# DeltaNet decays from shared operands: the sums of g, and the causal mask added in PSUM

## The chip, the cores and the metric

The kernel runs on one core of one Trainium2 chip. The metric is the device time of one execution in microseconds; the time of a kernel is the median of its runs.

## The reference

Two layers over 512 positions of width 1024, all in float32. Layer 0 mixes tokens with gated DeltaNet, layer 1 with a convolution module; each layer then attends to a memory of 256 positions and applies an MLP of width 4096. Only the gates and decays of the DeltaNet layer are changed:

```python
proj = h @ w_in                                   # q, k, v, z and 2 x 8 columns b_raw, a_raw
beta = jax.nn.sigmoid(b_raw)
g = -jnp.exp(a_log) * jax.nn.softplus(a_raw + dt_bias)     # log-decay, one per position and head
g_cum = jnp.cumsum(g, axis=-1)                    # within a chunk
diff = g_cum[..., :, None] - g_cum[..., None, :]
decay = jnp.exp(jnp.where(causal, diff, -jnp.inf))
lower = jnp.where(strict, einsum(k_beta, k) * decay, 0.0)   # I + lower is then solved
attn_intra = einsum(q, k) * decay
```

There are eight heads of width 128. The kernel works with chunks of 128 positions, four for each head.

## The kernel before, in words

Activations lie transposed: 128 channels on the partitions, 512 positions along the free axis. A large product in near-float32 precision is three matmuls of type float32r: each operand is split into a high and a low part (`h`, `l`), and `mm3` (lines 218 to 222) adds high x high, high x low and low x high in PSUM. Weights arrive by DMA as `raw` tiles of 128x1024; `wsplit` casts the high part `wh` on ScalarE (ACT) and subtracts the low part `wl` on VectorE (DVE).

The DeltaNet layer is written as a list `mains` of matmul pieces, most of 12 matmuls (half of one 128-column block of the projection), in the order `DN_ORDER`: k, q, z, v of heads 0 to 3, then of heads 4 to 7. `S.at(i, rank, f)` hangs side work on a piece `i`, and `run` emits it after that piece. The numbers at the end of the file (`T_STAT`, `T_DEC`, `K2`, `Q2`, `FS`, `DEC1`) say at which piece. The framework then orders each engine's instructions anew from this program, so an edit can move neighbours that it does not name. Each engine takes its own queue strictly in order.

The steps around the change:

- `mm_ab` (line 1112) interleaves the projection of the first k head with the 16 columns of alpha and beta: for each of 8 input tiles three matmuls of 512 columns for the head and three with 16 weight columns (`abh`, `abl`).
- `Norm.square`, `stat`, `spread`: the sum of squares over the channels (`sq` on DVE, `ssq` on TensorE), its root on ACT, and its spread `rb` over all partitions. All evictions of the projections multiply by `rb`.
- `gates` (line 338): `ab` times `rb`, four transposes to positions on the partitions, then some twenty small steps on DVE and three exponentials on ACT that give `g` and `beta`, 128x32 (8 heads x 4 chunks).
- `decay_in` (line 386): for each head GpSimd (POOL) forms `gi` = the triangle times `g`, 128x512; ACT and DVE split it into `gih` and `gil`.
- `decay` (line 393): for each head two matmuls of the other triangle with `gih` and `gil` give the sums of g between two positions; ACT takes the exponential, POOL sets the part above the diagonal to zero with a second product with the triangle. The result is `DtM[h]`, tile `dt`.
- `conv_head` (line 410): each head of q, k and v is multiplied by `rb` (`cv`, DVE), convolved over four positions (`cva`, by ACT, DVE, and with `cvq` also POOL), and goes through a silu on ACT (line 426).
- `k2` (line 434): transposes and the Gram matrix G of a k head; `bt` = G times the decay (DVE), scaled by `s_all` on POOL. `fs_in` gathers the diagonal blocks of `bt` into `DB` (ACT).
- `q2`, `q3`: the product of k and q times the decay (in place in `dt`), and the squares `sqq` of q for its norm.
- `fs_begin`, `fs_steps`, `fs_end`: for a group of four heads a transpose `FT` of `DB`, 31 dependent steps of forward substitution on DVE, and two transposes `TB`, `UB`.
- `mg_pre` to `mg_end`: the blocks are merged to full inverses (`mg`), with copies by ACT (`x0`) and POOL (`u0`).
- `rec`, `o_gate`, `o_norm`: the recurrence over the four chunks.

All PSUM tiles share eight banks, all 128x512 working tiles share `NSLOT` = 66 buffers. Small tiles come from the pool `sp`.

Of the kernel before, what the change touches and what calls it, by code (L numbers as in the profile page):

```python
# [8 lines left out]
F32 = mybir.dt.float32  # L9
# [5 lines left out]
P = 128  # L15
# [25 lines left out]
def tile_trunk(ctx, tc, xT, memT, prm_d, adt_d, bdw_d, fin_d, w_ab, w_kq, w_v, w_z, w_dno, w_pw1, w_pw2,  # L41
# [7 lines left out]
    up = ctx.enter_context(tc.tile_pool(name="up", bufs=NSLOT))  # L49
    sp = ctx.enter_context(tc.tile_pool(name="sp", bufs=16))  # L50
    psp = ctx.enter_context(tc.tile_pool(name="psp", bufs=8, space=bass.MemoryType.PSUM))
# [16 lines left out]
    def const(shape, s, dt=F32):  # L68
        return cp.tile(list(shape), dt, tag=s, name=s)

    def tt(e, o, a, b, op):
        e.tensor_tensor(out=o, in0=a, in1=b, op=op)  # L72
# [46 lines left out]
    for i in range(WARM):  # L119
# [6 lines left out]
                       base=0, channel_multiplier=1)  # L126
    tri_gt_r = const([P, P], "tri_gt_r", F32R)
    act.copy(tri_gt_r, tri_gt)
    ident4 = const([P, 32], "ident4")
# [197 lines left out]
    class DeltaNet:  # L327
        def __init__(self, norm):
            self.n, self.xs = norm, norm.xs
            for n, s in ((64, "abt"), (32, "beta"), (32, "g"), (96, "egd"), (32, "sek"), (32, "nk"),  # L330
                         (32, "s_all"), (32, "sdec"), (32, "s_neg"), (32, "sdec_neg"), (32, "ssq"), (4, "tok")):
                setattr(self, s, keepc(n, s))
            for s in ("GI", "DtM", "KT", "Kt", "Ai", "QT", "BT", "U", "VT", "VB", "Z", "OG", "ps", "M"):
                setattr(self, s, {})
# [50 lines left out]

        def decay_in(self, hs):
            for h in hs:
                gi = slot(s="gi")
                tt(pool, c4(gi), over_c(tri_le), over_i(self.g[:, h * 4:h * 4 + 4]), ALU.mult)
                self.GI[h] = split(gi, "gi")  # L390

        def decay(self, hs):
# [6 lines left out]
            for h in hs:  # L399
                gh, gl = self.GI.pop(h)  # L400
                ps = psum("dt")
                pe.matmul(ps, tri_gt_r, gh, start=True, stop=False)
                pe.matmul(ps, tri_gt_r, gl, start=False, stop=True)
                dt = slot(s="dt")
                act.activation(dt, ps, AF.Exp)
                tt(pool, c4(dt), c4(dt), over_c(tri_le), ALU.mult)
                self.DtM[h] = dt
# [687 lines left out]
    for b in range(4):  # L1095
        bs = slice(32 * b, 32 * b + 32)
        pool.tensor_copy(ident4[bs, :], ident[bs, bs])
    abh, abl = const([P, P], "abh", F32R), const([P, P], "abl", F32R)
    act.copy(abh, wab)
    tt(dve, abl, wab, abh.bitcast(F32), ALU.subtract)  # L1100
    n0 = Norm("dn_norm", eng=dve)
# [10 lines left out]
    def mm_ab():  # L1112
        w = wnext(("k", 0), 0)
        D.ps["ab"], D.ps["k", 0] = psum("ab"), psum("h")
        for k in range(KT):
            mm3(D.ps["k", 0], wk(w, k), n0.xs[k], k == 0, k == KT - 1)
            c = slice(16 * k, 16 * k + 16)
            mm3(D.ps["ab"][0:16, :], (abh[:, c], abl[:, c]), n0.xs[k], k == 0, k == KT - 1)

# [170 lines left out]
T_STAT = 2  # L1290
T_DEC = 10
NW = 3
# [110 lines left out]
```

## Time and profile before

| | us |
|---|---|
| median of 3 runs | 1588.56 (1587.7 to 1592.16) |
| profiled execution, its own time | 1589.25 |
| its span | 1587.5 |
| TensorE busy in the span | 1541.6 |
| DVE, ACT, POOL busy | 907.0, 656.9, 263.5 |

A line of a timeline has the start and length in us, the engine, the line of the kernel, the operation, the tile written and the tiles read, their shapes, how many such instructions are merged, and in brackets the time for which the engine was idle just before, with the instruction that ended that wait. A line of a group has the count, the busy time and the mean length in ns of one. Buffer numbers are left out of tile names. A row of stretches has the length, then for each engine its busy time and the number of its instructions, then the clock that TensorE was granted as a share of full speed, the busy share of the DMA engines and the GB/s that they moved.

### The profile page before, as it was taken

Reading aid. Unit: us, or ns where it says so; the run is one execution under the profiler, and the core shown is the slowest. Engines: PE = TensorE matmul, PEld = TensorE weight load, DVE = VectorE, ACT = ScalarE, POOL = GpSimd, SP = SyncE. Lnnn points to the kernel's source line nnn. Section 1 sums busy time; section 2 is a strip of 40 time slices with the busy share of each in tenths; the row PEclk is TensorE's granted clock in tenths of the full one; section 3 lists DMA queues with packets and bytes.
Section 4 is the critical chain, followed back from the end, with each engine's and each line's share of the span. In section 5 each row is a group of like instructions: output and inputs, shape, how many; then the busy total and the mean of one; then the engine's idle time right before and its main releaser. Section 6 shows DMA issues by size and latency. Waiting matters only on the chain.

```text
span 1587.5 us, 19586 instructions
## 1 busy us (share of the span) xinstructions
PE 1541.6 (97%) x7696; PEld 1298.6 (82%) x7696; DVE 907.0 (57%) x1288; ACT 656.9 (41%) x1004; POOL 263.5 (17%) x298
## 2 busy tenths in 40 slices
PE   9998997899999999999999999999999999999998
PEld 6777876798888888888888889888888888888886
DVE  6886878566455444343445599984545443443441
ACT  6656573745344443241324321173444432322332
POOL 1526333502111100000021316202012000000000
PEclk9999999899999999999999999999999999999999
DMA  5221113153222222322232422243212222223231
GB/s 180 67 73 60 54 42 105 52 175 107 93 66 67 87 100 93 104 96 93 96 104 93 137 88 91 73 164 101 85 41 93 93 98 101 94 93 105 95 106 53
DMA packets 46699, 147.57 MB, mean 93 GB/s; under 512 B 6288, under 2 KB 8976, under 8 KB 46608
## 3 DMA queue, kind: packets, MB, share of 16 engines
q1 hardware_dynamic: 46608, 146.33, 27.4%
q8 instruction: 60, 0.98, 0.2%
q14 instruction: 31, 0.25, 0.1%
HBM read 142.90 MB, written 2.10 MB: 91 GB/s over the span
## 4 chain that ended last, share of the span: by engine, by line
PE 85%; DVE 7%; ACT 3%; POOL 2%; issue 2%; DMA 0%; SPq 0%; DVEq 0%; POOLq 0%; ACTq 0%
PE up L220 7%; PE up L222 7%; PE up L221 7%; PE dn L220 6%; PE dn L222 6%; PE dn L221 6%; DVE ca L75 3%; PE q L220 2%; PE xo L221 2%; PE q L222 2%; PE q L221 2%; PE xo L222 2%; PE xo L220 2%; PE h L221 2%; PE pw L220 2%; PE pw L221 2%
## 5 line engine op out<-in xcount | busy, mean ns | idle before, releaser
L204 ACT CAST wh<-raw 128x1024 fp32r<-128x1024 f32 x248 | 260.5, 1052 | 705.8 <-PE dn L221 190.4
L72 DVE TENSOR_TENSOR wl<-raw,wh 128x1024 fp32r<-128x1024 f32 x248 | 312.1, 1260 | 129.7 <-ACT wh L204 123.9
L220 PE MATMUL up<-xh,wh 128*128 128x512 f32 x512 | 200.2, 391 | 0.0
L222 PE MATMUL up<-xh,wl 128*128 128x512 f32 x512 | 199.2, 389 | 0.0
L221 PE MATMUL up<-xl,wh 128*128 128x512 f32 x512 | 199.2, 389 | 0.0
L222 PE MATMUL dn<-uh,wl 128*128 128x512 f32 x448 | 174.3, 389 | 0.0
L220 PE MATMUL dn<-uh,wh 128*128 128x512 f32 x448 | 174.3, 389 | 0.0
L221 PE MATMUL dn<-ul,wh 128*128 128x512 f32 x448 | 174.3, 389 | 0.0
L72 DVE TENSOR_TENSOR h<-dn,h 128x512 f32<-128x512 f32 x56 | 41.8, 747 | 165.2 <-PE dn L222 165.2
L75 DVE SCALAR_TENSOR_TENSOR rl<-up,rb 128x512 f32<-128x512 f32 x64 | 44.2, 691 | 156.9 <-PE up L222 156.9
L72 POOL TENSOR_TENSOR tap<-ident,prm 128x512 f32<-128x512 f32 x45 | 61.9, 1406 | 329.6 <-PE up L222 263.8
L221 PEld LDWEIGHTS up<-xl,wh 128*128 128x128 f32 x512 | 96.1, 188 | 20.3 <-issue 0.5
L220 PEld LDWEIGHTS up<-xh,wh 128*128 128x128 f32 x512 | 96.1, 188 | 20.3 <-issue 0.5
L222 PEld LDWEIGHTS up<-xh,wl 128*128 128x128 f32 x512 | 96.1, 188 | 20.1
L222 PEld LDWEIGHTS dn<-uh,wl 128*128 128x128 f32 x448 | 84.1, 188 | 17.5
L220 PEld LDWEIGHTS dn<-uh,wh 128*128 128x128 f32 x448 | 84.1, 188 | 17.4
L221 PEld LDWEIGHTS dn<-ul,wh 128*128 128x128 f32 x448 | 84.1, 188 | 17.4
L72 POOL TENSOR_TENSOR sq<-sq,sq 128x512 f32<-128x512 f32 x30 | 49.9, 1664 | 252.7 <-ACT sq L295 167.8
L75 DVE SCALAR_TENSOR_TENSOR ca<-x,prm,ca 128x512 f32<-128x512 f32 x90 | 81.8, 910 | 2.1
L220 PE MATMUL h<-xh,wh 128*128 128x512 f32 x192 | 77.4, 403 | 2.1 <-ACT xh L288 2.1
L221 PE MATMUL h<-xl,wh 128*128 128x512 f32 x192 | 75.8, 395 | 0.6 <-DVE xl L75 0.6
L222 PE MATMUL h<-xh,wl 128*128 128x512 f32 x192 | 75.3, 392 | 0.0
(321 smaller groups left out, 3109.4 us busy)
## 6 DMA issues: line engine op xcount, KB each, us to landing
raw<-w_up SPq DMA_DIRECT2D x64, 512.0 KB, 3.4
raw<-w_dn SPq DMA_DIRECT2D x64, 512.0 KB, 3.5
raw<-w_pw SPq DMA_DIRECT2D x24, 512.0 KB, 3.5
raw<-w_kq SPq DMA_DIRECT2D x16, 512.0 KB, 3.6
raw<-w_k SPq DMA_DIRECT2D x16, 512.0 KB, 3.5
raw<-w_vv SPq DMA_DIRECT2D x16, 512.0 KB, 3.6
raw<-w_q SPq DMA_DIRECT2D x16, 512.0 KB, 3.4
raw<-w_o SPq DMA_DIRECT2D x16, 512.0 KB, 3.5
```

The source lines that it names most:

```text
L72: e.tensor_tensor(out=o, in0=a, in1=b, op=op)
L75: dve.scalar_tensor_tensor(out=o, in0=a, scalar=s, in1=b, op0=op0, op1=op1)
L204: act.copy(h, raw)
L220: pe.matmul(ps, wh, xh, start=first, stop=False)
L221: pe.matmul(ps, wh, xl, start=False, stop=False)
L222: pe.matmul(ps, wl, xh, start=False, stop=last)
```

## The change

*Decays.* The triangle product for each head goes, and with it `gi`, `gih`, `gil` and the mask product. One product of all heads' g with a triangle whose columns are taken relative to column 63 (`tri_mid`) gives the sums of g, head and chunk on the partitions, four copies one below the other; they are split into a float32r part and a rest (`V`). From `V` come one operand `R` for all heads (each chunk's sums, beside a pattern of ones) and one operand `L` for each group of four heads (a pattern that selects the head, beside the negative sums). The constant parts of `R` and `L` are copied on POOL (`decay_const`), the others written by DVE. For each head TensorE first writes -1e30 above the diagonal into PSUM (the identity times `later`, repeated for four chunks), then adds the product of the head's 128 columns of `L` with `R`; the exponential follows as before and gives zero above the diagonal. The first decays are emitted one piece later (`T_DEC` 11 instead of 10).

*Alpha and beta.* High and low weights stand side by side in one operand of 32 columns (`abp`): two matmuls for each input tile instead of three. The two halves of the result are added after the transposes.

The pool of small tiles has 13 buffers instead of 16.

```diff
-    sp = ctx.enter_context(tc.tile_pool(name="sp", bufs=16))
+    sp = ctx.enter_context(tc.tile_pool(name="sp", bufs=13))
...
-    tri_gt_r = const([P, P], "tri_gt_r", F32R)
-    act.copy(tri_gt_r, tri_gt)
+    ident_r = const([P, P], "ident_r", F32R)
+    act.copy(ident_r, ident)
+    later = const([P, P], "later", F32R)
+    ts(pool, later, tri_le, 1.0, ALU.subtract, 1e30, ALU.mult)
+    tri_mid = const([P, P], "tri_mid")
+    ts(pool, tri_mid, tri_le, tri_le[:, 63:64], ALU.subtract)
+    ind = const([P, 4], "ind")
+    dve.tensor_reduce(out=ind, in_=ident.rearrange("p (x c) -> p c x", c=4), op=ALU.add, axis=AX.X)
+    headm = const([P, 8], "headm")
+    headx = const([P, 32], "headx")
+    dve.tensor_reduce(out=headx, in_=ident.rearrange("p (x c) -> p x c", c=4), op=ALU.add, axis=AX.X)
+    dve.tensor_reduce(out=headm, in_=headx.rearrange("p (a h) -> p h a", h=8), op=ALU.add, axis=AX.X)
...
-            tt(dve, ab[0:16, :], self.ps.pop("ab")[0:16, :], rb[0:16, :], ALU.mult)
+            tt(dve, ab[0:32, :], self.ps.pop("ab")[0:32, :], rb[0:32, :], ALU.mult)
...
-                pe.transpose(ps_t[:, c * 16:(c + 1) * 16], ab[0:16, c * P:(c + 1) * P], ident[0:16, 0:16])
+                pe.transpose(ps_t[:, c * 32:(c + 1) * 32], ab[0:32, c * P:(c + 1) * P], ident[0:32, 0:32])
...
-            dve.tensor_copy(abt.rearrange("p (x c) -> p x c", c=4),
-                            ps_t[:, 0:64].rearrange("p (c x) -> p x c", c=4))
+            abp = ps_t[:, 0:128].rearrange("p (c x) -> p x c", c=4)
+            a3 = abt.rearrange("p (x c) -> p x c", c=4)
+            dve.tensor_copy(a3, abp[:, 16:32])
+            tt(dve, a3, abp[:, 0:16], a3, ALU.add)
...
-        def decay_in(self, hs):
-            for h in hs:
-                gi = slot(s="gi")
-                tt(pool, c4(gi), over_c(tri_le), over_i(self.g[:, h * 4:h * 4 + 4]), ALU.mult)
-                self.GI[h] = split(gi, "gi")
+        def decay_const(self, gq):
+            if gq == 0:
+                self.R = slot(F32R, "R")
+                pool.tensor_copy(c4(self.R)[64:128], over_i(ind)[64:128])
+            self.L[gq] = slot(F32R, "L")
+            pool.tensor_copy(c4(self.L[gq])[0:64], over_i(headm[:, 4 * gq:4 * gq + 4])[0:64])
+
+        def decay_sums(self):
+            grep = slot(s="grep")[:, 0:P]
+            dve.tensor_copy(grep.rearrange("p (a x) -> p a x", a=4), over_c(self.g))
+            ps = psum("ct")
+            pe.matmul(ps[:, 0:P], grep, tri_mid, start=True, stop=True)
+            v = self.V
+            act.copy(v, ps[:, 0:P])
+            for a in (1, 3):
+                rs = slice(32 * a, 32 * a + 32)
+                tt(dve, v[rs], ps[rs, 0:P], v[rs].bitcast(F32), ALU.subtract)
+            tt(dve, c4(self.R)[0:64], over_c(v.bitcast(F32))[0:64], over_i(ind)[0:64], ALU.mult)
+
+        def decay_in(self, gq):
+            stt(c4(self.L[gq])[64:128], over_c(self.V.bitcast(F32))[64:128], -1.0,
+                over_i(headm[:, 4 * gq:4 * gq + 4])[64:128], ALU.mult, ALU.mult)
...
-                gh, gl = self.GI.pop(h)
                 ps = psum("dt")
-                pe.matmul(ps, tri_gt_r, gh, start=True, stop=False)
-                pe.matmul(ps, tri_gt_r, gl, start=False, stop=True)
+                pe.matmul(c4(ps), ident_r, over_c(later), start=True, stop=False)
+                pe.matmul(ps, self.L[h // 4][:, h % 4 * P:h % 4 * P + P], self.R, start=False, stop=True)
                 dt = slot(s="dt")
                 act.activation(dt, ps, AF.Exp)
-                tt(pool, c4(dt), c4(dt), over_c(tri_le), ALU.mult)
                 self.DtM[h] = dt
...
-            mm3(D.ps["ab"][0:16, :], (abh[:, c], abl[:, c]), n0.xs[k], k == 0, k == KT - 1)
+            xh, xl = n0.xs[k]
+            pe.matmul(D.ps["ab"][0:32, :], abp[:, 32 * k:32 * k + 32], xh, start=k == 0, stop=False)
+            pe.matmul(D.ps["ab"][0:16, :], abp[:, 32 * k:32 * k + 16], xl, start=False, stop=k == KT - 1)
...
-    S.at(T_STAT + 5, 5, D.decay_in, [0, 1, 2, 3])
+    S.at(0, 4, D.decay_const, 0)
+    S.at(T_DEC - 1, 2, D.decay_sums)
+    S.at(T_DEC - 1, 3, D.decay_in, 0)
     S.at(T_DEC, 2, D.decay, [0, 1])
     S.at(T_DEC + 1, 2, D.decay, [2, 3])
+    S.at(DEC1[0] - 2, 5, D.decay_const, 1)
+    S.at(DEC1[0], 5, D.decay_in, 1)
     for i, hh in enumerate(([4, 5], [6, 7])):
-        S.at(DEC1[i], 5, D.decay_in, hh)
         S.at(DEC1[i] + 2, 2, D.decay, hh)
...
-T_DEC = 10
+T_DEC = 11
```

More of the change, by code (lines that the diff above doesn't have):

```diff
@@ L332, in __init__ @@
                 setattr(self, s, keepc(n, s))
-            for s in ("GI", "DtM", "KT", "Kt", "Ai", "QT", "BT", "U", "VT", "VB", "Z", "OG", "ps", "M"):
+            self.V = cp.tile([P, P], F32R, tag="gsum", name="gsum")
+            self.L = {}
+            for s in ("DtM", "KT", "Kt", "Ai", "QT", "BT", "U", "VT", "VB", "Z", "OG", "ps", "M"):
                 setattr(self, s, {})
@@ L1097, in tile_trunk @@
         pool.tensor_copy(ident4[bs, :], ident[bs, bs])
-    abh, abl = const([P, P], "abh", F32R), const([P, P], "abl", F32R)
-    act.copy(abh, wab)
-    tt(dve, abl, wab, abh.bitcast(F32), ALU.subtract)
+    abp = const([P, 2 * P], "abp", F32R)
+    ab3 = abp.rearrange("p (k x) -> p k x", k=KT)
+    act.copy(ab3[:, :, 0:16], wab.rearrange("p (k x) -> p k x", k=KT))
+    tt(dve, ab3[:, :, 16:32], wab.rearrange("p (k x) -> p k x", k=KT), ab3[:, :, 0:16].bitcast(F32), ALU.subtract)
     n0 = Norm("dn_norm", eng=dve)
@@ L1116, in mm_ab @@
             mm3(D.ps["k", 0], wk(w, k), n0.xs[k], k == 0, k == KT - 1)
-            c = slice(16 * k, 16 * k + 16)
-            mm3(D.ps["ab"][0:16, :], (abh[:, c], abl[:, c]), n0.xs[k], k == 0, k == KT - 1)
+            xh, xl = n0.xs[k]
+            pe.matmul(D.ps["ab"][0:32, :], abp[:, 32 * k:32 * k + 32], xh, start=k == 0, stop=False)
+            pe.matmul(D.ps["ab"][0:16, :], abp[:, 32 * k:32 * k + 16], xl, start=False, stop=k == KT - 1)
     mains.extend([mm_ab, lambda: None, lambda: None, lambda: None])
```

## The prediction

> **What bounds the kernel now.** I read the page first, then the busy time of each engine in stretches of 50 us, then TensorE's timeline for every idle gap, then the timelines of the engines that ended those gaps.
>
> ```profile
> span 1587.5 us, 19586 instructions
> PE 1541.6 (97%) x7696; PEld 1298.6 (82%) x7696; DVE 907.0 (57%) x1288; ACT 656.9 (41%) x1004; POOL 263.5 (17%) x298
> 50.00:100.00 50.00, 45.66 (x244) 38.42 (x243) 37.53 (x63) 33.62 (x58) 22.30 (x37) 0.97 0.17 56
> 250.00:300.00 50.00, 33.63 (x171) 27.02 (x169) 31.83 (x50) 33.44 (x59) 28.14 (x39) 0.90 0.15 53
> 600.00:650.00 50.00, 50.00 (x222) 41.42 (x221) 21.43 (x25) 15.85 (x20) 0.00 (x0) 1.00 0.28 95
> ```
>
> The columns after the length are the busy us of PE, PEld, DVE, ACT and POOL, then the granted clock. From 350 us on TensorE has nothing to wait for (row 600: 222 matmuls in 50 us, 0.225 us each), and the change touches nothing there. Nearly all of the 46 us in which it is idle lie in the DeltaNet stage, before 310 us, and the clock is lower there too. These are its gaps, with their length and releaser in brackets:
>
> ```profile
> 45.56 0.50 PE L403 MATMUL dt<-gil,tri_gt_r 128*128 128x512 f32 x1 [0.41 <-DVE gil L72]
> 48.98 0.50 PE L403 MATMUL dt<-gil,tri_gt_r 128*128 128x512 f32 x1 [1.54 <-DVE gil L72]
> 75.44 1.05 PE L480 MATMUL ssq<-ones,sqq 128*128 128x1 f32 x8 [0.72 <-ACT sqq L468]
> 78.44 0.50 PE L251 MATMUL z<-wh,xh 128*128 128x512 f32 x1 [0.45 <-DVE dt L72]
> 86.90 1.05 PE L480 MATMUL ssq<-ones,sqq 128*128 128x1 f32 x8 [3.17 <-ACT sqq L468]
> 136.40 3.91 PE L546 MATMUL mg<-x,bt 128*128 128x96 f32 x17 [4.93 <-ACT x L537]
> 200.65 1.26 PE L630 MATMUL vn<-r,u 128*128 128x128 f32 x8 [1.01 <-DVE r L75]
> 209.57 1.13 PE L658 MATMUL o<-vn,dt 128*128 128x128 f32 x8 [0.89 <-ACT cva L426]
> 221.68 1.16 PE L466 MATMUL ai<-cva,cva 128*128 128x128 f32 x8 [1.92 <-ACT cva L426]
> 278.96 1.35 PE L546 MATMUL mg<-x,bt 128*128 128x96 f32 x5 [11.19 <-POOL msq L72]
> ```
>
> So work taken off TensorE, or off any other engine, is worth only what it takes out of these gaps.
>
> **What goes: the decay work on POOL, ACT and DVE.**
>
> ```profile
> L72 POOL TENSOR_TENSOR gi<-tri_le,g x8: 1037/1265/2017, 41.3 to 189.2; 128x512 f32<-128x512 f32 x8
> L72 POOL TENSOR_TENSOR dt<-dt,tri_le 128x512 f32<-128x512 f32 x8 | 11.9, 1516 | 8.7 <-ACT dt L405 8.7
> ```
>
> For each head one product on POOL (median 1.27 us), a cast on ACT, a subtraction on DVE and the mask on POOL (1.52) go: some 22 us of POOL, half of it in each group of four heads. TensorE's decay matmuls stay two of 512 columns for each head. What the masks did to the first group is seen in these rows:
>
> ```profile
> 53.18 6.37 POOL L72 TENSOR_TENSOR dt<-dt,tri_le 128x512 f32<-128x512 f32 x4 [4.80 <-ACT dt L405]
> 59.55 1.28 POOL L72 TENSOR_TENSOR cva<-cva,cvq 128x512 f32<-128x512 f32 x1
> 62.44 0.63 ACT L426 ACTIVATE cva<-cva 128x512 f32<-128x512 f32 x1 [2.89 <-DVE cva L75]
> 77.82 0.63 ACT L426 ACTIVATE cva<-cva 128x512 f32<-128x512 f32 x1 [1.95 <-DVE cva L75]
> 86.23 1.13 ACT L468 ACTIVATE sqq<-cva 128x512 f32<-128x512 f32 x2
> 92.48 1.25 DVE L500 STREAM_TRANSPOSE FT<-DB 128x1024 f32<-128x1024 f32 x1 [1.70 <-ACT DB L493]
> ```
>
> The convolution's addition for the first q head stands on POOL behind four masks; DVE, then ACT's silu at 62.44, wait for it. From there a chain that goes to and fro between ACT, POOL and DVE ends in the square `sqq` at 86.23, for which TensorE idles 3.17 us, and in the transpose FT at 92.48, with which the forward substitution on DVE begins.
>
> In the changed program's order the exponentials feed the product with G directly. I take the decay matmuls at about 53.5 us (below). Two exponentials, the scaling and cvq on ACT (0.5 + 0.5 + 0.62 + 0.62) end at 55.8, the addition on POOL (1.28) at 57.1, two steps on DVE (0.67 each) at 58.5; ACT still has two exponentials, a square, a copy and a table load, so the silu starts at about 59.3 instead of 62.44: 3.1 us earlier. From there ACT's own queue is the chain, by the new order and each operation's own duration: silu, square and copy 1.7, a wait of 0.5 for cv, scaling and cvq 1.35, wh 1.05, eight DB copies 3.4, silu 0.63, wh 1.05 and scaling and cvq 1.35 end at 70.3; POOL's addition (1.28) and three steps on DVE (1.95) bring the third q head's silu to 73.6 instead of 77.82, 4.2 us earlier. One more head of the same kind, in which bt and the addition no longer queue on POOL, brings 4.9. The square then ends at 86.23 + 0.53 - 4.9 = 81.9. TensorE, which came there at 83.73, comes at about 83.3 when the two gaps before it (0.72 and 0.45) are gone and the start is later. So all three gaps go, 4.3 us. With 3.1 us alone the square would end at 83.7, and 0.4 us would stay.
>
> After that gap the clock falls:
>
> ```profile
> 88.73 0.63 PE L251 MATMUL z<-wh,xh 128*128 128x512 f32 x1
> 91.72 0.45 PE L252 MATMUL z<-wl,xh 128*128 128x512 f32 x1
> ```
>
> Seven matmuls in 2.99 us are 0.43 us each instead of 0.225; some 1.6 us are lost there. The Trainium skill ("TensorE: Matmul & The Clock Gate", Part 1) says that the clock is halved after an idle window of about 3.4 us and that the windows run freely. The trace agrees as to the halving, but a gap of 3.17 us was enough here.
>
> With that TensorE would reach the merges (136.40) 5.2 us earlier; FT, and the substitution behind it, comes 4.9 us earlier. The later of the two decides: -4.9 us.
>
> **What is added at the start.** On DVE three small reductions stand after the first wl and ahead of the eight xl; on POOL two copies of 64x512 (R and L) wait for them and run beside the xl.
>
> ```profile
> 9.24 5.39 DVE L75 SCALAR_TENSOR_TENSOR xl<-x,prm,xh 128x512 fp32r<-128x512 f32 x8
> 53.17 5.23 DVE L75 SCALAR_TENSOR_TENSOR cva<-cv,prm,cva 128x512 f32<-128x512 f32 x3
> 58.33 0.67 DVE L453 TENSOR_REDUCE sm<-sqk 128x4 f32<-128x512 f32 x1
> 20.26 0.68 DVE L72 TENSOR_TENSOR sq<-sq,sq 128x512 f32<-128x512 f32 x1
> 22.51 0.95 PE L306 MATMUL ssq<-ones,sq 128*128 128x1 f32 x8
> 26.18 1.10 PE L316 MATMUL rb<-dg,ones 128*128 128x512 f32 x2
> L538 POOL COPY u<-UB 32x128 f32<-32x128 f32 x32 | 12.7, 396 | 8.5 <-DVE UB L518 7.0
> L1097 POOL COPY ident<-ident 32x32 f32<-32x32 f32 x4 | 0.8, 204 | 0.1
> ```
>
> A reduction over 512 elements took 0.67, one over 128 at most a third and some fixed time: 0.65 us for the three, bounds 0.4 and 2.0. The two POOL copies, by the line through 204 ns at 32 and 396 ns at 128 elements, are 1.16 us each. DVE's steps took 0.67 us each by themselves (row 9.24) and 1.74 each while POOL's masks ran (row 53.17), so I let each copy hold up one xl by about 1 us: 2 us, bounds 0 and 2.3. The Trainium skill ("SBUF — State Buffer", Who interferes with whom) says that a DVE instruction with two SBUF inputs and a GpSimd instruction that reads SBUF lock each other out for a whole instruction. The trace's 1.74 against 0.67 agrees, and by that rule alone the copies speak against the change at this place, and the removed masks for it.
>
> DVE's sums of squares follow the xl without a break, so the last, at 20.26, ends at 20.86 + 2.65 = 23.5, and ssq comes 1.0 us later than at 22.51. TensorE is there by then, although its 8 saved `ab` matmuls (1.8 us) would have brought it to 20.7: **that saving is lost behind the sum of squares**. In the new order one wl stands between rstd and dg, and dg ends about when rb's turn comes; I take rb, and all behind it, as 1.1 us later, bounds -1.8 and +2.5. Without the 2 us of the conflict rb would keep its old time, and the sum below would be -8.6 instead of -7.5.
>
> **The new wait for g.**
>
> ```profile
> 33.07 1.21 DVE L72 TENSOR_TENSOR wl<-raw,wh 128x1024 fp32r<-128x1024 f32 x1
> 41.06 0.18 DVE L72 TENSOR_TENSOR g<-sm,sm 128x32 f32<-128x32 f32 x1
> 44.09 0.31 PE L395 MATMUL gsum<-g,ones 128*128 128x32 f32 x2
> ```
>
> The new order puts four convolution steps (0.67), one cv (0.6) and two wl (1.14) more ahead of g: 5.6 us, so g comes at 46.7, or 47.8 with the later start, and `grep` at 48.1. TensorE meets `ct` 12 matmuls after the old gsum: 44.09 + 2.7 + 1.1 = 47.9. Adding up each operation's own waits gives up to 1.7 us of waiting; I take 1.3, in place of 1.95 (0.41 + 1.54), and `ct` costs at most 0.3 of work. Then ACT copies V, and DVE does cv, wl, two subtractions, R and L (0.6 + 1.14 + 0.4 + 1.3 = 3.4 us), while TensorE does ct, gsum, two `later` and 12 other matmuls (about 4 us): hidden, with 0.6 us to spare. Without that cover, every us of delay in g is a us on TensorE, and the next G, bt and DB queue behind it.
>
> **The order at the merges.**
>
> ```profile
> 142.85 0.63 ACT L426 ACTIVATE cva<-cva 128x512 f32<-128x512 f32 x1 [1.08 <-POOL cva L72]
> 145.96 2.88 PE L558 MATMUL mg<-u,w 128*96 128x96 f32 x32
> ```
>
> POOL's copies into u0 now stand earlier: 16 instead of 9 ahead of the last addition of this v head, 7 x 0.396 = 2.8 us. ACT's silu (142.85) and the four copies w behind it come so much later, at 145.6 and 146.2, and the first w ends at 146.7 where TensorE needs it at 145.96: +0.7 us, bounds 0 and 2.8.
>
> **The second group of heads.**
>
> ```profile
> 203.00 2.54 POOL L72 TENSOR_TENSOR dt<-dt,tri_le 128x512 f32<-128x512 f32 x2 [0.60 <-ACT dt L405]
> 206.82 0.75 DVE L75 SCALAR_TENSOR_TENSOR cva<-cv,prm,cva 128x512 f32<-128x512 f32 x1 [4.18 <-POOL cva L72]
> ```
>
> Two masks stood ahead of the addition for which DVE idled 4.18 us, and two gil stood ahead of r. By the new order r comes 3.6 us and this step 4 us earlier, more than the gaps at 200.65, 209.57 and 221.68 (3.8 us). I take 3.3, bounds 1.5 and 3.8, since the last gap also hangs on two table loads. The second substitution moves along, so the 11.19 us at 278.96 stay. L for this group is one POOL copy and one DVE step (0.67) in a stretch where TensorE does not wait.
>
> **Sum.** -4.9 + 0.7 - 3.3 = -7.5 us; the start (+1.1) and the wait for g (-0.4 net) are in the first term. The profiled execution took 1589.25 us, its span and 1.75 us around it, 0.7 above the median of 1588.56. From the median: 1581.1 us. A measurement of this kernel tells about 0.3% (4.8 us) from no change; the forecast is beyond that.
>
> **Rivals.**
>
> *Given back* (chance 0.2): only the 3.1 us seen directly reach FT, and the second group gives half of its gaps. For it: the chain to 92.48 crosses three engines and each crossing can bind. Against it: POOL is nearly empty there. -3.1 + 0.7 - 1.7 = -4.1: 1584.5, no change that can be told.
>
> *The wait for g becomes the bound* (0.08), slower. Row 41.06: g moves behind steps that themselves wait for ACT, where two table loads stand. If it comes 10 us later than I take, TensorE idles 11 us at `ct`, the clock halves for two windows (2 x 1.6 us), and all decays, and with them the whole chain to FT, start 10 us later: -7.5 + 10 + 3.2 = +5.7, or 1594.3. It turns slower than before at about 4.3 us of delay.
>
> *More* (0.1): no port conflict at the start, no wait for g, no late w, and FT still earlier: -7.5 - 1.1 - 1.3 - 0.7 - 1.5 = -12.1: 1576.5.
>
> *The mask matmul is slow* (inside the range): its moving operand repeats one 128-column tile four times. If that read went at half rate, 8 x 0.225 = 1.8 us more: 1582.9.
>
> **Numbers.** The forecast has 0.62. Its own range is 1577 to 1584.5; the rivals on either side widen it to 1576 to 1588, which leaves out the slower case and the tail. Faster by over 0.3%: most of the 0.62 and all of *more*, 0.66. Same: *given back* and the forecast's edge, 0.25. Slower: 0.09.
>
> **What would show it.** Right: no gap of TensorE for sqq near 82 us, clock 1.0 between 80 and 100 us, FT near 87.6, and gaps under 1 us between 190 and 220; ssq about 1 us later than at 22.51 despite fewer matmuls; a gap of 1 to 2 us before `ct`. Wrong: a gap before `ct` or before the matmul of L and R of over 4 us, FT not before 90, or the gap at the merges grown by what the first group gained.

## The result, and the profile after

The changed kernel takes 1584.24 us (median; 1582.56 to 1584.99), the kernel before 1590.07 us beside it (1587.70 to 1592.16). The ratio is 0.9964, 95% interval 0.9952 to 0.9976: 5.8 us or 0.36% faster. The forecast was 1581.1 us, range 1576 to 1588, "faster by over 0.3%" the likeliest. The profiled execution of the changed kernel took 1584.79 us, its span 1583.1.

The head of its page, and its busy time in the three stretches of 50 us that matter (columns as in the prediction: length, PE, PEld, DVE, ACT, POOL, granted clock):

```profile
span 1583.1 us, 19556 instructions
...
PE 1539.9 (97%) x7690; PEld 1300.1 (82%) x7690; DVE 897.3 (57%) x1290; ACT 652.5 (41%) x997; POOL 239.5 (15%) x287
...
50.00:100.00 50.00, 49.73 (x275) 42.52 (x274) 36.00 (x74) 33.80 (x59) 15.23 (x32) 1.00 0.19 64
100.00:150.00 50.00, 40.95 (x201) 34.97 (x200) 32.93 (x53) 27.99 (x52) 27.12 (x40) 0.86 0.17 56
250.00:300.00 50.00, 35.14 (x185) 29.74 (x184) 32.45 (x50) 36.70 (x68) 27.41 (x39) 0.76 0.13 42
```

From 50 to 100 us TensorE now waits for hardly anything (45.66 us busy before, 49.73 now, clock 1.00). The stretch with the first merges, 100 to 150, is worse than it was, and the clock at the second merges is lower, 0.76 against 0.90. TensorE's gaps, with length and releaser in brackets:

```profile
26.37 1.13 PE L326 MATMUL rb<-dg,ones 128*128 128x512 f32 x2 [0.54 <-DVE dg L72]
...
47.72 0.46 PE L415 MATMUL ct<-tri_mid,grep 128*128 128x128 f32 x2 [0.74 <-DVE grep L413]
...
80.97 1.05 PE L513 MATMUL ssq<-ones,sqq 128*128 128x1 f32 x8 [0.27 <-ACT sqq L501]
...
130.44 6.57 PE L579 MATMUL mg<-x,bt 128*128 128x96 f32 x32 [6.48 <-ACT x L570]
...
142.35 4.53 PE L591 MATMUL mg<-u,w 128*96 128x96 f32 x32 [2.57 <-ACT w L581]
...
216.77 1.16 PE L499 MATMUL ai<-cva,cva 128*128 128x128 f32 x8 [1.51 <-ACT cva L459]
...
274.02 1.99 PE L579 MATMUL mg<-x,bt 128*128 128x96 f32 x8 [11.18 <-POOL msq L72]
```

The three gaps of the first group between 75 and 87 us (0.72, 0.45 and 3.17 us) have shrunk to one of 0.27, and the second group has kept one of three, 1.51 instead of 1.92 us. Two gaps have grown: 4.93 to 6.48 us at the first merges, and 2.57 us before `mg<-u,w`, where there was none. So the first merges start 6.0 us earlier (136.40 to 130.44), but the first `vn` behind them only 2.0 us earlier (171.39 to 169.37).

### The profile page after: what moved, and what is told of

Same layout as the page of the kernel before. It is cut to its first block, busy times and chain, and to the rows that moved or that the text cites. A ratio compares the mean times of both kernels' runs of the same rounds, so it can differ in the third digit from the quotient of the medians.

```text
span 1583.1 us, 19556 instructions
## 1 busy us (share of the span) xinstructions
PE 1539.9 (97%) x7690; PEld 1300.1 (82%) x7690; DVE 897.3 (57%) x1290; ACT 652.5 (41%) x997; POOL 239.5 (15%) x287
## 4 chain that ended last, share of the span: by engine, by line
PE 79%; DVE 11%; ACT 4%; issue 2%; POOL 2%; SPq 1%; DMA 1%; DVEq 0%; POOLq 0%; ACTq 0%
PE up L230 7%; PE up L232 7%; PE up L231 7%; PE dn L232 6%; PE dn L231 6%; PE dn L230 6%; DVE ca L75 3%; PE q L230 2%; PE xo L231 2%; DVE wl L72 2%; PE q L231 2%; PE q L232 2%; PE xo L232 2%; PE xo L230 2%; PE pw L230 2%
```

## The experiments

Each line of this table is one profile, in us, with the median and the ratio of all timed runs. "FT" is counted from the start of `rb`, which takes the start of the kernel out of it. "vn" is the first vn behind the first merges, "ai" the matmul at which the gap of 1.5 to 3.4 us stands in the second group, "to mg" the way from there to the second merges, and "half" the time at half clock between 205 and 245 us, as 2 x (1 - clock) added up over slices of 1 us. Each ratio is to the kernel before as it ran beside that kernel (medians 1589.84 to 1591.41 us), so it tells more than the medians of different rows. `rb` stands between 24.4 and 27.2 us in these profiles, and "vn" and "ai" still hold that difference. A profile is one run, and not always a typical one.

| kernel | median | ratio, 95% | FT | vn | ai | to mg | half |
|---|---|---|---|---|---|---|---|
| before | 1590.07 | 1 | 66.30 | 171.39 | 221.68 | 57.28 | 0 |
| changed | 1584.24 | 0.9964 (0.9952-0.9976) | 60.19 | 169.37 | 216.77 | 57.25 | 0 |
| changed, again | 1583.02 | 0.9957 (0.9944-0.9970) | 60.17 | 168.50 | 215.88 | 57.25 | 0 |
| only the operand for alpha and beta | 1588.25 | 0.9997 (0.9988-1.0007) | 61.68 | 169.41 | 219.66 | 62.07 | 10.2 |
| only the decays | 1582.33 | 0.9954 (0.9942-0.9966) | 60.05 | 167.83 | 215.23 | 57.26 | 0 |
| before, mask in PSUM | 1586.85 | 0.9987 (0.9978-0.9995) | 64.55 | 169.31 | 218.96 | 58.89 | 3.4 |
| changed, masks back on POOL | 1588.54 | 0.9992 (0.9983-1.0002) | 62.79 | 172.15 | 220.15 | 58.85 | 3.4 |
| u copies behind the additions | 1582.29 | 0.9952 (0.9939-0.9965) | 60.15 | 166.85 | 214.27 | 57.26 | 0 |
| reductions earlier | 1582.70 | 0.9955 (0.9941-0.9969) | 60.19 | 167.50 | 214.90 | 57.26 | 0 |
| TensorE kept busy | 1586.35 | 0.9978 (0.9969-0.9987) | 60.17 | 170.68 | 218.08 | 57.57 | 0 |
| nk behind DB | 1584.92 | 0.9962 (0.9949-0.9975) | 58.30 | 169.18 | 218.48 | 61.18 | 10.2 |
| before, nk behind DB | 1600.41 | 1.0057 (1.0042-1.0072) | 65.04 | 176.18 | 228.39 | 62.22 | 13.7 |
| three edits | 1582.77 | 0.9958 (0.9943-0.9972) | 58.27 | 167.01 | 216.31 | 56.35 | 0 |
| three edits, 16 columns | 1586.34 | 0.9969 (0.9958-0.9980) | 58.27 | 165.95 | 215.25 | 61.17 | 10.2 |

### One part of the change alone

Only the operand for alpha and beta, on the kernel before:

```diff
-            mm3(D.ps["ab"][0:16, :], (abh[:, c], abl[:, c]), n0.xs[k], k == 0, k == KT - 1)
+            pe.matmul(D.ps["ab"][0:32, :], abp[:, 32 * k:32 * k + 32], xh, start=k == 0, stop=False)
+            pe.matmul(D.ps["ab"][0:16, :], abp[:, 32 * k:32 * k + 16], xl, start=False, stop=k == KT - 1)
```

> The kernel before, with only the alpha and beta weights as one 32-column operand; the decays stay as they were. Theory (the 8 saved matmuls, 1.8 us, hide behind DVE's sum of squares, and the new order, in which more convolution steps stand ahead of g and 16 u copies ahead of the v head's silu, costs something): no gain, 0 to +4 us against the kernel before, and the gap before the first decay matmuls grows. Rival (TensorE bounds the start, so the saving is kept): -1.8 us against the kernel before.

Measured: no gain that can be told (0.9997), as the theory said. But FT came at 86.78 us, which nobody expected, and TensorE has no gap at all for `sqq`, although the masks and `gi` are all still there. POOL's masks, then ACT's timeline:

```profile
50.63 6.66 POOL L72 TENSOR_TENSOR dt<-dt,tri_le 128x512 f32<-128x512 f32 x4 [1.83 <-ACT dt L407]
...
84.96 1.77 ACT L495 COPY DB<-bt 32x128 f32<-32x128 f32 x4 [0.55 <-POOL bt L72]
86.75 0.63 ACT L428 ACTIVATE cva<-cva 128x512 f32<-128x512 f32 x1
87.40 1.28 ACT L577 ACT_TABLE_LOAD   x1
```

In this program's order the last copies into DB stand ahead of the silu and of the square root `nk` with its table load. In the kernel before and in the changed one they stand behind two table loads. FT is the end of ACT's queue, and what else is in that queue counts. So a new order, with no work taken from POOL, brought FT 4.6 us earlier (counted from `rb`) and took out the gap for `sqq`; this limits what the runs below can say of the change. What this kernel had won at `ai` (2.0 us) it lost again on the way to the second merges, 62.07 us instead of 57.28; more on that below.

Only the decays: the changed kernel with `abh` and `abl`, three matmuls for each k, as before (the diff above the other way round).

> The changed kernel with the alpha and beta weights as two 16-column operands again, three matmuls for each k. Theory (the gain is the decays' alone): within 1.5 us of the changed kernel, so 4 to 6 us faster than the kernel before. Rival (half the gain or more came from the alpha and beta operand): at most 3 us faster than the kernel before.

Measured: the whole gain, 0.9954. The decays, with the order that comes with them, make it alone. `mg<-u,w` has no gap here:

```profile
140.63 2.88 PE L589 MATMUL mg<-u,w 128*96 128x96 f32 x32
```

With 16 columns POOL's order has 9 u copies ahead of the v head's last addition again, not 16, and `ai` comes 0.7 to 1.5 us earlier than in the two profiles of the changed kernel. In these profiles the smaller operand costs time by the order that comes with it; the medians don't tell the two kernels apart.

### Masks and operands taken apart

On the kernel before, `gi`, `gih` and `gil` stay, and the mask moves to PSUM:

```diff
+                pe.matmul(c4(ps), ident_r, over_c(later), start=True, stop=False)
-                pe.matmul(ps, tri_gt_r, gh, start=True, stop=False)
+                pe.matmul(ps, tri_gt_r, gh, start=False, stop=False)
                 pe.matmul(ps, tri_gt_r, gl, start=False, stop=True)
                 act.activation(dt, ps, AF.Exp)
-                tt(pool, c4(dt), c4(dt), over_c(tri_le), ALU.mult)
```

> The kernel before, with gi, its cast and its subtraction as they were, but the mask added in PSUM by a third matmul for each head and the product with tri_le on POOL gone; 8 matmuls of 0.225 us (1.8 us) more than before. Theory (the masks on POOL held the chain to FT): FT, at 92.5 us before, comes 4 to 6 us earlier, the 3.17 us gap for sqq goes, and the time is 3 to 6 us under the kernel before. Rival (the gain came from the shorter preparation gi, gih, gil): no gain, between the kernel before and +1.8 us.

The other way round, on the changed kernel:

```diff
                 act.activation(dt, ps, AF.Exp)
+                tt(pool, c4(dt), c4(dt), over_c(tri_le), ALU.mult)
```

> The changed kernel with the product with tri_le put back on POOL after each exponential (it changes no value, since what it zeroes is zero); every other instruction is in the changed kernel's order on every engine. Eight masks, 1.5 us each. Theory (masks): FT, at 86.6 us in the changed kernel, is 3 to 5 us later, half of the second group's gaps come back, and the time is 3 to 6 us over the changed kernel. Rival (the shared operands made the gain): within 1 us of the changed kernel.

The first gained 0.13% and the second lost most of the gain. The gap for `sqq`, FT, and the gap of the second group, with the masks gone and `gi` kept:

```profile
83.34 1.05 PE L484 MATMUL ssq<-ones,sqq 128*128 128x1 f32 x8 [0.59 <-ACT sqq L472]
...
88.93 1.25 DVE L504 STREAM_TRANSPOSE FT<-DB 128x1024 f32<-128x1024 f32 x1 [1.73 <-ACT DB L497]
...
218.96 1.69 PE L470 MATMUL ai<-cva,cva 128*128 128x128 f32 x8 [1.91 <-ACT cva L430]
```

With the masks back on POOL and the shared operands kept:

```profile
53.34 2.53 POOL L72 TENSOR_TENSOR dt<-dt,tri_le 128x512 f32<-128x512 f32 x2 [5.67 <-ACT dt L439]
55.84 1.29 POOL L72 TENSOR_TENSOR cva<-cva,cvq 128x512 f32<-128x512 f32 x1
...
83.90 1.87 PE L514 MATMUL ssq<-ones,sqq 128*128 128x1 f32 x8 [2.88 <-ACT sqq L502]
...
220.15 1.90 PE L500 MATMUL ai<-cva,cva 128*128 128x128 f32 x8 [1.92 <-ACT cva L460]
```

Two masks ahead of the addition are enough to bring back the gaps of 2.88 and 1.92 us. Up to 330 us, every engine of this kernel shows the changed kernel's instructions in the changed kernel's order, with eight masks more on POOL. So the price of the masks is measured by itself, and the theory of this run was right in the main: FT is 2.6 us later counted from `rb`, the gap for `sqq` 2.6 us longer, and most of the gain is gone (0.9992 against 0.9964). Of the second group's gaps only 0.4 us came back.

On the kernel before, the masks' going also took most of the gap for `sqq` (3.17 to 0.59 us), but FT, counted from `rb`, came only 1.75 us earlier, and the time only 2.1 us under: less than that theory had, more than its rival. With the shared operands and the masks kept, FT came 3.5 us earlier than before, and 6.1 us with both parts. Those 3.5 us are not shown to be the work of `gi`, `gih` and `gil`: that kernel and the kernel before differ in order too, and the kernel with only the operand for alpha and beta, with all the work of the kernel before, came 4.6 us earlier. What the shared operands give as work, apart from the order, stays open. The smaller pool of small tiles and `T_DEC` were not tried alone either.

In the times the two parts give less still (0.0013 and 0.0008 of 1590 us, 2.1 and 1.3 of 5.8 us, and the second can't be told from nothing). With one part only, the gap before `ai` stays at 1.9 us, and both profiles, of runs above their medians, have half clock behind it.

### Where the gain was given back: the merges

The u copies queued behind the third v head's last addition, in the changed kernel (shortened; the condition for the second group is left out, and every other instruction keeps its order):

```diff
             for b in range(4):
                 bs = slice(32 * b, 32 * b + 32)
-                pool.tensor_copy(c4(u0)[bs, :, bs], UBv[bs, n, :])
+                with tc.issue_after(self.la[2]):    # that head's last addition
+                    pool.tensor_copy(c4(u0)[bs, :, bs], UBv[bs, n, :])
```

> The changed kernel with POOL's 16 copies u<-UB queued behind the last addition of the third v head; nothing else is moved on any engine. Theory (the copies ahead of that addition make ACT's silu, w and TensorE late): silu, at 141.2 us, comes before 137, the 2.57 us gap before mg<-u,w goes, and the time is 1 to 2.6 us under the changed kernel. Rival (another wait takes its place, on u or at vt): within 0.7 us of the changed kernel.

First POOL and ACT in the changed kernel, then in this one:

```profile
130.20 3.48 POOL L571 COPY u<-UB 32x128 f32<-32x128 f32 x8 [5.43 <-DVE UB L551]
133.75 1.26 POOL L72 TENSOR_TENSOR cva<-cva,cvq 128x512 f32<-128x512 f32 x1
...
139.90 1.26 POOL L72 TENSOR_TENSOR cva<-cva,cvq 128x512 f32<-128x512 f32 x1
...
141.20 0.63 ACT L459 ACTIVATE cva<-cva 128x512 f32<-128x512 f32 x1 [5.40 <-POOL cva L72]
141.73 1.61 ACT L581 ACTIVATE w<-mg 128x384 f32<-128x384 f32 x4
```

```profile
129.65 0.95 POOL L522 MEMSET DB<- 128x1024 f32 x1 [4.65 <-DVE UB L551]
130.56 3.96 POOL L453 TENSOR_TENSOR cva<-cva,cvq 128x512 f32<-128x512 f32 x3
134.46 8.07 POOL L579 COPY u<-UB 32x128 f32<-32x128 f32 x16
...
135.31 0.63 ACT L459 ACTIVATE cva<-cva 128x512 f32<-128x512 f32 x1
...
142.59 0.92 PE L599 MATMUL mg<-u,w 128*96 128x96 f32 x8 [0.72 <-POOL u L579]
```

In the changed kernel POOL idles 5.43 us for UB, because the copies are ahead, and then makes the silu wait. With the additions ahead, silu comes 5.9 us earlier and the gap goes; 0.72 us come back, as POOL is now late with the last u. Against the second profile of the changed kernel, `vn` and `ai` are 1.65 and 1.61 us earlier. So the theory held at its place. The median is 0.7 us lower (1582.29 against 1583.02), which can't be told from nothing; this profile spent 23.9 us at half clock at the second merges, the other 13.7.

### The start

The three reductions of the constants queued ahead of the first wl, where DVE waits for its first weights (shortened):

```diff
-        tt(dve, lo, raw, h.bitcast(F32), ALU.subtract)
+        with tc.issue_after(headm_ins):     # the first wl only
+            tt(dve, lo, raw, h.bitcast(F32), ALU.subtract)
```

> The changed kernel with the three reductions on DVE queued ahead of the first wl, where DVE waits for its first weights, and so R and L on POOL earlier. Theory (reductions 0.72 us and port conflict 0.55 us stand on the chain to ssq): the gap of 0.63 us before ssq goes, rb comes 0.6 to 1.2 us earlier, and the time is 0.5 to 1.2 us under the changed kernel. Rival (the chain from g or FT hides the start): within 0.3 us of the changed kernel.

```profile
8.95 5.38 DVE L75 SCALAR_TENSOR_TENSOR xl<-x,prm,xh 128x512 fp32r<-128x512 f32 x8
...
25.39 1.12 PE L330 MATMUL rb<-dg,ones 128*128 128x512 f32 x2 [0.57 <-DVE dg L72]
```

The eight xl take 5.38 us, as before the change; with the R and L copies beside them they take 5.94. `rb` comes 1.05 us earlier than in the second profile of the changed kernel (26.44), and `vn` and `ai` with it, 1.0 us each. So the start is on the path, us for us, as the theory had it. The median moved by 0.3 us, which is the rival's number and can't be told from nothing: the profile of this kernel spent 17.1 us at half clock at the second merges, the other 13.7.

### The changed kernel once more, and TensorE kept busy

> The changed kernel once more, for a second profile. If half-clock stretches follow free-running windows, gaps are the same to 0.1 us, but the stretches begin and last differently by whole windows of about 3.4 us, and the span moves with them by 0.5 to 2 us. If they follow the gaps alone, both profiles show the same stretches.

The same program, two profiles, in three stretches with half clock; first the one above, then the second:

```profile
143.00:147.00 4.00, 4.00 (x29) 3.96 (x28) 0.25 (x1) 4.00 (x8) 2.44 (x4) 0.57 0.00 0
265.00:285.00 20.00, 10.64 (x45) 9.42 (x46) 5.32 (x4) 12.79 (x25) 14.68 (x27) 0.57 0.08 27
293.00:304.00 11.00, 8.85 (x56) 8.51 (x56) 7.91 (x13) 7.41 (x16) 5.58 (x6) 0.53 0.31 97
```

```profile
143.00:147.00 4.00, 4.00 (x36) 3.67 (x35) 0.21 (x1) 4.00 (x8) 2.44 (x4) 1.00 0.00 0
265.00:285.00 20.00, 10.67 (x54) 8.62 (x54) 4.43 (x4) 13.40 (x26) 15.56 (x28) 0.74 0.05 20
293.00:304.00 11.00, 9.75 (x94) 9.21 (x95) 8.86 (x14) 8.34 (x17) 4.99 (x5) 0.84 0.30 97
```

From 20 us on the gaps agree to 0.7 us (0.1 us was expected), the half-clock stretches do not. The span is 1580.0 against 1583.1 us, and nearly all of the 3.1 us lies behind those stretches: 0.9 us at `vn`, 2.2 us behind the second merges.

Then idle products in TensorE's gaps at the merges, in the changed kernel (shortened):

```diff
             ps = psum("mg")
+            for _ in range({0: 24, 7: 44}.get(h, 0)):      # in mg_w; 9 and 12 in mg_y
+                pe.matmul(c4(ps), ident_r, over_c(later), start=True, stop=True)
```

> The changed kernel with TensorE kept busy in its gaps at the merges: 24 idle products of 512 columns before the first mg<-x,bt, 9 before mg<-u,w, 44 and 12 at the same places of the second group; they write a part of PSUM that the next product overwrites, and take 5.4, 2.0, 9.9 and 2.7 us at 0.225 us each, less than the gaps of 6.48, 2.57, 11.18 and 3.35 us. Theory (half clock behind the gaps is on the path): clock 1.0 from 126 to 147 us, the first mg<-x,bt takes 4 us instead of 6.57 and mg<-u,w 2.9 instead of 4.53, and the time is 3 to 8 us under the changed kernel. Rival (the chain through ACT and POOL sets the merges, whatever the clock): within 1 us of the changed kernel.

```profile
130.66 1.10 PE L581 MATMUL mg<-x,bt 128*128 128x96 f32 x8 [1.18 <-ACT x L570]
...
135.75 1.10 PE L581 MATMUL mg<-x,bt 128*128 128x96 f32 x8 [0.59 <-ACT x L570]
...
143.59 4.53 PE L595 MATMUL mg<-u,w 128*96 128x96 f32 x32 [1.87 <-POOL X L531]
```

At full clock eight products take 1.10 us, and TensorE then waits 0.6 us for the next four x: the group ends at 136.85, and at half clock at 137.0 (130.44 + 6.57) and 137.5 in the two profiles of the changed kernel, well before w comes in any of them. The theory falls for this place: ACT's copies set it, and half clock costs nothing there. For the rest the run decides little, since the idle products also changed ACT's order (a wh stands ahead of w, and `mg<-u,w` comes 1.2 us later, at half clock again). The kernel was 3.3 us slower than the changed one.

### FT earlier still

`nk` queued behind the last copy into DB, on the changed kernel (shortened):

```diff
-            act.activation(self.nk[:, hs], self.sek[:, hs], AF.Sqrt)
+            with tc.issue_after(last_db_copy):
+                act.activation(self.nk[:, hs], self.sek[:, hs], AF.Sqrt)
```

> The changed kernel with ACT's square root nk, and the two table loads around it, queued behind the last copy into DB in both groups. Theory (after the masks, ACT's own queue is the chain to FT, and the table loads are the last thing on it): FT, at 86.6 us, comes at 84.5; in the second group the 1.51 us gap before ai goes; the time is 1.5 to 3.5 us under the changed kernel. Rival (given back at the merges, where the order on POOL puts all 16 u copies ahead of the additions): within 0.7 us of the changed kernel.

```profile
84.77 1.23 DVE L534 STREAM_TRANSPOSE FT<-DB 128x1024 f32<-128x1024 f32 x1
...
128.47 0.72 ACT L448 ACTIVATE cva<-cv,prm 128x512 f32<-128x512 f32 x1 [4.68 <-DVE cv L72]
...
130.94 6.75 ACT L571 COPY x<-TB 32x128 f32<-32x128 f32 x16
...
132.31 6.25 PE L580 MATMUL mg<-x,bt 128*128 128x96 f32 x32 [8.24 <-ACT x L571]
...
218.48 1.26 PE L499 MATMUL ai<-cva,cva 128*128 128x128 f32 x8 [2.96 <-ACT cva L459]
```

FT comes 1.8 us earlier, and the merges start 1.8 us later than in the changed kernel. DVE ends the substitution earlier, ahead of the v head's cv, and the scaling that needs this cv stands on ACT ahead of the x copies. And in the second group the silu still stands behind `nk`, which is now later: the gap before `ai` is 2.96 us instead of 1.5. The rival was right as to the time (0.9962 against 0.9964 and 0.9957), but not as to the cause: it is ACT's order at the merges, not the u copies on POOL. The profiled run took 1590.46 us, the other four 1583.83 to 1585.22, so the 10.2 us at half clock behind this gap are not the rule.

The same move on the kernel before:

> The kernel before with the same move of nk. Theory: here the last bt on POOL (it ends at 89.4 us) holds FT, not the table loads, so FT comes 1 to 1.5 us earlier (92.5 to 91.2), the 1.92 us gap before ai goes, and the time is 1 to 3 us under the kernel before. Rival (the order on ACT alone, without the change, gives the change's gain): 4 us or more under the kernel before, FT at 88 or earlier.

It is slower by 0.57%. FT stands at 92.06 us (1.3 us earlier, counted from `rb`) and DB waits 1.45 us for bt, as expected. But the first merges start at 140.06 us, 3.7 us later than before, with the scaling ahead of the x copies on ACT as above; the gap before `ai` is 3.38 us, and 13.7 us at half clock follow it. The theory was right at FT alone, and its rival was wrong: this one move in ACT's order doesn't give the change's gain.

Three edits at once (reductions, nk, and the u copies, here also ahead of the memsets for the second group), with 32 and with 16 columns:

> The changed kernel with three edits at once: the reductions ahead of the first wl, nk behind the last copy into DB, and the u copies behind the third v head's additions (and ahead of the memsets for the second group). Theory (each is on the path): -1.0 at the start, -2.0 at FT, -1.6 to -2.3 at the first merges and -1.5 in the second group, so 5 to 7 us under the changed kernel, less what half-clock stretches give back: 1576 to 1579. Rival (each uncovers the same next wait): less than 3 us under the changed kernel.

> The same three edits with the alpha and beta weights as two 16-column operands again (8 matmuls more, 1.8 us of TensorE at the start). Theory (DVE still sets ssq and rb, with gaps of 0.3 and 0.6 us there): at most 1 us slower than with the 32-column operand, and ssq at most 1 us later. Rival (with DVE relieved, TensorE bounds the start): 1.5 to 2 us slower.

The first is 0.9958, no better than the changed kernel, as its rival said: it gains 1.5 us at `vn` against the second profile of the changed kernel, and loses it before `ai`, where the gap is now 2.97 us. With 16 columns `rb` stands at 25.39 instead of 25.40 us, as the theory had it, and `vn` and `ai` even come 1.06 us earlier. (The pair is not quite fair: TensorE spent 3.4 us of the start at half clock with 32 columns, and none with 16.) And yet the median is 3.6 us higher, twice what the rival had. The clock from 220 to 225 us, in the first and then in the second, and the second merges of each:

```profile
220.00:225.00 5.00, 5.00 (x32) 4.42 (x32) 4.75 (x9) 1.27 (x5) 1.42 (x2) 1.00 0.25 80
...
272.66 1.99 PE L593 MATMUL mg<-x,bt 128*128 128x96 f32 x8 [10.74 <-POOL msq L72]
```

```profile
220.00:225.00 5.00, 5.00 (x16) 4.28 (x17) 3.35 (x8) 0.00 (x0) 0.40 (x2) 0.50 0.16 45
...
276.42 1.99 PE L591 MATMUL mg<-x,bt 128*128 128x96 f32 x8 [10.75 <-POOL msq L72]
```

The gap is 2.97 and 2.96 us. One profile has no half clock behind it, the other 10.2 us, with 16 matmuls in 5 us instead of 32, and arrives 3.8 us later after having been 1.1 us ahead. Of the six runs with 32 columns, two took 1586.9 and 1587.4 us, so the higher median need not come from the operand.

No kernel run here beats the changed one by more than the measurement tells. The lowest medians, 1582.29 and 1582.33 us, belong to the kernel with the additions ahead and to the one with the decays alone; the intervals of both overlap the changed kernel's.

## Why the prediction was right, and where its sizes were off

**The bound was read rightly.** The change was worth what it took out of TensorE's gaps, less what it added to them. The gap for sqq went (3.17 to 0.27 us), the clock is 1.00 from 50 to 100 us, and nothing behind 350 us moved: from the last `vn` to the end it is 1241.7 us in the kernel before and in both profiles of the changed one. FT came at 86.56 us; the forecast had 87.6. Counted from `rb` it had 6.0 us (4.9, and 1.1 for the start), and 6.1 was measured.

**The chain to FT.** The forecast walked the new order operation by operation and had the first q head's silu at 59.3 and the third's at 73.6 us:

```profile
57.89 0.63 ACT L459 ACTIVATE cva<-cva 128x512 f32<-128x512 f32 x1
...
72.45 0.63 ACT L459 ACTIVATE cva<-cva 128x512 f32<-128x512 f32 x1 [1.98 <-DVE cva L75]
...
86.56 1.25 DVE L533 STREAM_TRANSPOSE FT<-DB 128x1024 f32<-128x1024 f32 x1 [1.75 <-ACT DB L526]
```

Both come 1.2 to 1.4 us earlier than forecast, since the first product of L and R does (51.9 instead of 53.5 us). Its reason, the work that goes, is shown for the masks only: of the 6.1 us at FT they make 1.75 us when they go alone and 2.6 us when they go last. The rest comes with the shared operands, and whether by their work or by the order that the program got with them is not shown.

**The start.** "+1.1 us for rb and all behind it": `rb` came 0.2 us later (26.37 against 26.18), or 0.8 us counted from the first weights, which came 0.6 us earlier in that profile (wh at 6.43 instead of 7.03). The size was nearly right, by steps that were not. The forecast put ssq 1.0 us later than at 22.51; it came at 21.68, 0.2 us earlier counted from wh. The port conflict was put at 2 us and took 0.55, the POOL copies at 1.16 us each and took 0.61 and 0.95. Reductions and conflict together cost 1.27 us: the kernel with only the operand for alpha and beta, with the same first wh at 6.43, has its `rb` at 25.10. Nor is the operand's saving "lost behind the sum of squares": in that kernel ssq comes 1.5 us earlier than before, counted from wh, and `rb` 0.5. The other 1.0 us go to a step that the forecast named and gave no price, the wl between rstd and dg. Here it is in the changed kernel, where TensorE then waits 0.54 us for dg:

```profile
24.50 1.21 DVE L72 TENSOR_TENSOR wl<-raw,wh 128x1024 fp32r<-128x1024 f32 x1
```

**The wait for g.** 1.3 us forecast (1 to 2 among its signs), 0.74 measured, g at 47.05 (47.8 forecast), and TensorE doesn't wait between `ct` and the matmul of L and R. *The wait for g becomes the bound* did not come. Nor is *the mask matmul slow*: successive decay matmuls start 0.23 us apart, the repeated tile at the same rate as any other.

**The merges: the term that was mis-sized.** "+0.7 us, bounds 0 and 2.8." From the start of the first merges to `mg<-u,w`, where silu and w stand, the kernel before takes 9.56 us and the changed kernel 11.91 and, in its second profile, 11.90: 2.35 us, within the bounds and three times the forecast. The place and the mechanism were named rightly, u copies ahead of the addition, then silu, then w, and the run with the copies behind the additions shows it: 9.77 us. What was missed is that POOL also starts later: counted from the start of the merges, silu comes 4.3 us later than before and not 2.8. POOL's first u copy stood 1.3 us ahead of the merges before (135.08 and 136.40), and 0.24 us now.

From the start of the merges to the first `vn` the loss is larger, 3.9 us (34.99 to 38.93) and 3.0 us (38.03) in the second profile, above the upper bound. The rest comes after that wait: 1.6 us in the first profile, in which `mg<-u,w` itself ran at half clock (4.53 instead of 2.93 us), and 0.7 in the second, with a wait of 0.49 us before `vt`. With only the decays, `mg<-u,w` has no gap, and 1.38 us of waiting stand before `vt` instead.

**The second group.** -3.3 us forecast; from the `kS` near 194 us, 2.0 us earlier than before, to `ai`, 4.9 us earlier, it is -2.9. The two table loads that the forecast named did keep the last gap, at 1.51 us; among its signs it had all gaps between 190 and 220 us under 1 us. The 11.19 us before the second merges stayed, 11.18.

**The sum.** -7.5 us forecast, -5.8 measured between the medians; the two profiles of the changed kernel took 1584.79 and 1581.70 us against 1589.25: -4.5 and -7.6. In its own terms:

| | forecast | first profile | second profile |
|---|---|---|---|
| to the start of the first merges | -4.9 | -6.0 | -5.9 |
| first merges, to `vn` | +0.7 | +3.9 | +3.0 |
| second group, `vn` to `ai` | -3.3 | -2.9 | -2.9 |
| behind `ai` | 0 | +0.5 | -1.7 |

The last row and most of the difference in the second are the clock, for which the forecast had no term beyond the 1.6 us behind the gap for sqq. That the sum came within 1.7 us is in part luck: the first term gained 1.0 us more than forecast, the second lost 2.3 to 3.2 us more, and two profiles of one program differ by 3.1 us.

*Given back* had 1584.5 us, and 1584.24 was measured, so the time alone does not tell it from the forecast. Its mechanism did not come: more than 3.1 us reached FT, and the second group gave 2.9 us, not half. What was given back went at the first merges.

## What to carry to other kernels

Work taken off a side engine is worth only what it takes out of the bounding engine's gaps; here one half of the edit gave about a third of the time or less. When an edit shifts the order of instructions, follow each copy that moves ahead of an addition or a table load to its next user: the gain that was given back at the merges and the loss in the runs that moved `nk` came from such order and not from the work itself. Order can also give what is credited to the work: before a gain is put down to work that went, run a kernel with the new order and the old work, or, as with the masks, put the work back into the new order. And compare two profiles of the same kernel before explaining 3 us: a place name such as the first `vn` tells more than the end of the span.

## What the runs showed of the hardware

**Half clock comes in whole windows, and not always.** In every profile the time at half clock in one place is a multiple of 3.4 us: 6.8, 10.2 or 13.7 us at the first merges (3.4 with the idle products), 6.8 to 27.3 at the second, and 0, 3.4, 10.2 or 13.7 behind the gap before `ai`. With `nk` at its old place the way from `ai` to the second merges is 57.25 to 57.28 us without it (57.57 with the idle products), 58.85 and 58.89 with 3.4 us, and 62.07 with 10.2 us; with `nk` behind DB, 56.35 without it and 61.17 and 61.18 with 10.2 us. So about half of the stretch is lost where TensorE has work. Gaps of 1.49 to 1.53 us were followed by none of it in six profiles; of eight with 1.9 to 3.4 us, six had it. That a shorter gap is safe is not shown: elsewhere a gap of 1.78 us (kernel before with the mask in PSUM, at 47.2 us) and two of 1.34 and 1.85 us close together (only the operand for alpha and beta, before 50.5 us) were each followed by 3.4 us at half clock.

The Trainium skill ("TensorE: Matmul & The Clock Gate", Part 1) gives a free-running window of about 3.4 us, an idle one halving the clock and a busy one restoring it. The multiples agree, and so does the free run: gaps of 2.97 and 2.96 us were followed by none and by 10.2 us. What the runs add is that half clock followed gaps of 1.78 to 1.92 us, well under a window, and that TensorE stayed at half clock for 5 us in which its row (220 to 225 us, above) shows it busy all the time.

**A POOL addition stretches one DVE step each.** In the changed kernel's substitution, neighbouring steps of nearly the same size, with one of POOL's additions (110.83 us, 1.44 us long) beside the second:

```profile
110.74 0.39 DVE L72 TENSOR_TENSOR X<-X,fst 128x231 f32<-128x231 f32 x1
111.16 1.36 DVE L72 TENSOR_TENSOR fst<-FT,X 128x220 f32<-128x220 f32 x1
```

The DVE step then takes about as long as the addition. At the start the R and L copies (0.61 and 0.95 us) run beside the first two xl, which take 0.95 and 1.09 us instead of 0.74, and the eight of them lost 0.55 us together.
